# Turned q and k of the second half of the heads in two buffers, fetched two feature tiles ahead; apply of the first half three units behind the scores

## The chip, the core and the metric

The kernel runs on one core of one Trainium2 chip. The metric is the time of one execution on the device, in microseconds. The engines named below are TensorE (PE, matmuls), VectorE (DVE), ScalarE (ACT), GpSimd (POOL) and SyncE (SP); SP and POOL here mostly issue DMAs. Each engine takes its instructions in the order in which they stand in its own program, and waits at an instruction until the semaphores that it names have come.

## The reference

One layer of a hybrid encoder on 512 tokens of 1024 features, all in float32:

```python
x = x + 0.5 * swiglu(rmsnorm(x), w_ffn1)
h = rmsnorm(x)
xr, g, q, k, v, ga, gb = split(h @ w_in)        # 7 x 1024 columns
A = (rglru_forward(conv(xr)) + rglru_backward(conv(xr))) * gelu(g)
B = neighbourhood_attention(qk_norm(q), qk_norm(k), v, rpb)
x = x + (sigmoid(ga) * A + sigmoid(gb) * B) @ w_out
x = x + 0.5 * swiglu(rmsnorm(x), w_ffn2)
```

The attention has 16 heads of 64 features on a grid of 8 rows by 64 columns. A query sees all 8 rows and a window of 16 columns, with a learned bias `rpb`. The part that the change touches is this attention, and some buffers of the recurrent part (rglru).

## The kernel before

**Matmuls in three products.** Activations lie with features on partitions, 8 tiles of 128 features by 512 tokens. Each operand of a matmul is cut into a high and a low part (`split`, line 138 on), and a product is taken as high times high, low times high, high times low. A weight chunk is loaded by `load_w` (line 159): SP issues one DMA of 128x1024 floats into `wraw` (3 buffers, L163), ACT makes `wh` from it (L145) and DVE `wl` (L148, 4 buffers each), and PE then runs 24 matmuls of 512 columns on it (L172 to L174), 8 feature tiles by 3 products.

**Two kinds of work side by side.** The columns of the projection are computed chunk by chunk. Between the matmuls of a chunk generators ("lanes") are advanced at rates from the table `RATE`: `lru` for the recurrent part, `att` for the heads, `tail` for applies that are left over, `prep` for the norm of q and k, `v` for v. Within that a scheduler sets the final order on each engine by priority and by when a buffer is free. So a change of a buffer count moves instructions on every engine.

**The heads.** `heads(hf, ...)` handles half `hf` of the heads, 8 heads in 4 feature tiles `fi` of two heads each. For a tile, `start(fi)` makes `qh`, `ql`, `kh`, `kl` (ACT L960, DVE L962, ACT L963, DVE L965). `scores` runs the matmuls of q with k (PE L988), adds the bias and takes the maximum (DVE L1008), takes the exponential on ACT (L1015), the reciprocal of the sum (DVE L1017) and scales (ACT L1020). `ship` turns p on DVE (L1029, L1030) into `pt`, SP writes it to DRAM as `pd` (L1032), and POOL gathers it back, turned, into `PT` (L1036, four DMAs, 5 buffers). `apply` multiplies PT with v on PE (L1051) into a PSUM buffer, and ACT copies it out as `att` (L1061).

In half 0 a unit is half the columns of a tile (8 units), in half 1 a whole tile (4 units). `ATT_LAG` says how many units the apply of a tile stands behind its scores, 4 in half 0 and 2 in half 1; what is left at the end of a half goes to the lane `tail`.

**q and k of half 1** are normed in token layout, turned in blocks of 32 and written to DRAM as `qd` (L919). `fetch(qd, fi)` reads a tile back into `xqk` (four DMAs of SP, L932), which has one buffer: `fetch(0)` is called when `qd` is complete, and `start(fi)` calls `fetch(fi + 1)` behind the reads of tile fi. The buffers of the tags `xqk` and `PT` serve the recurrent part earlier in the program, for its cut inputs `ch` and `cl` (L728) and some of its `th` (L766); other `th` are in the common pool of large buffers.

**Around the change** PE runs the chunks of the columns for the gates (lines 1113 to 1124), which load from `wg`, and between them the scores and applies of both halves.

Of the kernel before, what the change touches and what calls it, by code (L numbers as in the profile page):

```python
# [9 lines left out]
F32 = mybir.dt.float32  # L10
F32R = mybir.dt.float32r
# [5 lines left out]
P = 128  # L17
T = 512
# [8 lines left out]
NCB, QC = 4, 16  # L27
# [33 lines left out]

GB_BATCH = (range(0, 4), range(4, 6), range(6, 7), range(7, 8))

ATT_LAG = 4, 2

LRU_PLAN = [
    ("root", range(4), range(39, 47)),
# [24 lines left out]
def block_kernel(ctx: ExitStack, tc, a, out):  # L92
# [4 lines left out]
    big = ctx.enter_context(tc.tile_pool(name="big", bufs=1))  # L97
# [10 lines left out]
    def nm(s):  # L108
        uid[0] += 1
        return f"{s}_{uid[0]}"  # L110
# [140 lines left out]
    def hold(i):  # L251

        after(i, mark["mm"])
        return i
# [454 lines left out]
    def lru():  # L709
        got, evicted, cuts, wts, fwd = {}, [], {}, {}, {}  # L710

        run = [None, None, None]

        def act(kind, i):
            hold(i)
            if kind == "tanh":
                kind = "exp" if run[0] == "sqrt" else run[0]
            if kind != run[0]:
                run[0], run[2] = kind, run[1]
            if run[2] is not None:  # L720
                after(i, run[2])
            run[1] = i

        def fetch(f):
            wts[f] = load_w(a["wgate"][f], 2 * P)

        def cut(f):
            cuts[f] = tuple(big.tile([P, T], F32R, tag="PT", bufs=5, name=nm(n)) for n in ("ch", "cl"))  # L728
            split(xc[f], *cuts[f])

        def gates(f):


            ps = [[aux_t() for _ in range(2)] for _ in range(2)]
            W, X = wts.pop(f), cuts.pop(f)
            mm = None
            for d in range(2):
                c = slice(d * P, (d + 1) * P)
                for w, x in ((0, 1), (1, 0), (0, 0)):
                    for b in range(2):  # L740
                        o = slice(b * HD, (b + 1) * HD)
                        prev, mm = mm, nc.tensor.matmul(  # L742
                            ps[d][b], W[w][o, c], X[x][o], start=x == 1, stop=w + x == 0)
                        if prev is not None:
                            after(mm, prev)
                        elif evicted:
                            after(mm, evicted[-1], True)
            for d in range(2):
                q = C_BG + f * 4 + d * 2
                both = pair_t()  # L750
                for b in range(2):
                    i = nc.scalar.activation(both[:, b], ps[d][b], AF.Sigmoid, bias=small[:, q + b : q + b + 1])
                    act("sigmoid", i)
                evicted.append(i)

                r, ix = (big_t(n="gate") for _ in range(2))
                for g, t in enumerate((r, ix)):
                    for b in range(2):
                        nc.gpsimd.dma_start(t[b * HD : (b + 1) * HD], both[g * HD : (g + 1) * HD, b])
                got[f, d] = r, ix  # L760

        def use(f, d):
            r, ix = got[f, d]
            hold(nc.vector.tensor_tensor(ix, ix, xc[f], ALU.mult))
            if d == 1 and f < 3:
                th = big.tile([P, T], F32, name=nm("th"), **(dict(tag="xqk", bufs=1) if f == 0 else dict(tag="PT", bufs=5)))  # L766
            else:
                th = big_t(n="th")
            act("tanh", nc.scalar.activation(th, r, AF.Tanh, scale=sp4[:, f * 2 + d : f * 2 + d + 1]))
            got[f, d] = r, ix, th  # L770


        def decay(f, d):
            r, ix, _ = got[f, d]
            act("exp", nc.scalar.activation(r, r, AF.Exp, scale=sn8[:, f * 2 + d : f * 2 + d + 1]))
            nc.vector.scalar_tensor_tensor(ix, r, 1.0, ix, ALU.add, ALU.mult)

        def root(f, d):
            _, ix, th = got[f, d]
            act("sqrt", nc.scalar.activation(th, th, AF.Sqrt))  # L780
            nc.vector.tensor_tensor(ix, ix, th, ALU.mult)

        def scan(f, d):
            av, ix, th = got.pop((f, d))
            if d == 0:
                fwd[f] = th
                i = hold(nc.vector.tensor_tensor_scan(th, av, ix, 0.0, ALU.mult, ALU.add))
            else:
                i = hold(nc.vector.tensor_tensor_scan(th[:, ::-1], av[:, ::-1], ix[:, ::-1], 0.0, ALU.mult, ALU.add))
            if "kl" in mark:  # L790
                after(i, mark["kl"])
            if d == 1:
                nc.vector.tensor_tensor(fwd[f], fwd[f], th, ALU.add)
                A[f] = fwd[f]

        plan = {}
        for fn, fs, steps in LRU_PLAN:
            units = list(fs) if fn in ("fetch", "cut", "gates") else [(f, d) for f in fs for d in range(2)]
            for u, step in zip(units, steps, strict=True):
                plan.setdefault(step, []).append((fn, u))  # L800
        do = dict(fetch=fetch, cut=cut, gates=gates, use=use, decay=decay, root=root, scan=scan)
        for step in range(max(plan) + 1):
            for fn, u in plan.get(step, []):
                do[fn](*(u if isinstance(u, tuple) else (u,)))
            yield
# [93 lines left out]
    def norm_qk(raws, st, qd):  # L899

        rq = tiny.tile([P, 2, NCB, 8], F32, tag="rq", name=nm("rq"))
        for w in range(2):
            for j in range(NCB):
                hold(nc.vector.tensor_scalar(rq[:, w, j, :], st[:, w, j, :], 1.0 / HD, epsv[:, j : j + 1],
                                             ALU.mult, ALU.add))
        hold(nc.scalar.activation(rq, rq, AF.Sqrt))
        nc.vector.reciprocal(rq, rq)
        yield
        for j in range(NCB):
            for w in range(2):  # L910
                t = raws[w][j].rearrange("p (h d) -> p h d", d=HD)
                hold(nc.vector.tensor_tensor(t, t, rq[:, w, j, :].unsqueeze(2).to_broadcast([P, 8, HD]), ALU.mult))
            if qd is not None:
                t2 = pair_t().rearrange("p a b -> p (a b)")
                for w in range(2):
                    nc.vector.transpose(
                        t2.rearrange("p (c f w i) -> p w f c i", c=NCB, f=4, w=2)[:, w],
                        raws[w][j].rearrange("p (f c i) -> p f c i", c=NCB, i=32))
                nc.sync.dma_start(qd[j], t2)  # L919
                yield  # L920
            elif j % 2 == 1:
                yield
        if qd is not None:
            yield
            fetch(qd, 0)

    xs = {}

    def fetch(qd, fi):
        t = xs[fi] = big.tile([P, NCB * NCB, 2, 32], F32, tag="xqk", bufs=1, name=nm("xqk"))  # L930
        for c in range(NCB):
            nc.sync.dma_start(  # L932
                t[c * 32 : (c + 1) * 32].rearrange("p g w i -> p g (w i)"),
                qd.rearrange("j (a i) c f x -> c f i (j a) x", a=NCB)[c, fi])

    def heads(hf, raws, qd):
# [6 lines left out]
        def start(fi):  # L943
# [19 lines left out]
            hold(nc.scalar.activation(k_of(kh), xk, AF.Copy))  # L963
            with tc.high_priority():
                mark["kl"] = nc.vector.tensor_tensor(k_of(kl), xk, k_of(kh.bitcast(F32)), ALU.subtract)  # L965
            if hf == 1 and fi < 3:
                fetch(qd, fi + 1)
            grid = lambda t: t.rearrange("p (r c) -> p r c", r=ROWS)
            qk[fi] = qh, ql, grid(kh), grid(kl)

# [52 lines left out]
        def ship(fi, n2):  # L1023

            outer, inner = soft.pop((fi, n2))
            t = big.tile([P, NCB, 7, 32], F32, tag="pt", bufs=2, name=nm("pt"))
            sub = lambda b, n: b[:, : n * P].rearrange("p (q c i) -> p q c i", q=n, i=32)
            to = t.rearrange("p c q i -> p q c i")
            nc.vector.transpose(to[:, 4:], sub(outer, 3))  # L1029
            nc.vector.transpose(to[:, :4], sub(inner, 4))  # L1030
            d = dram.tile([P, NCB, 7 * 32], F32, tag="pd", bufs=4, name=nm("pd"))
            nc.sync.dma_start(d, t.rearrange("p c q i -> p c (q i)"))  # L1032
            PT = big.tile([P, NCB, 7, 32], F32, tag="PT", bufs=5, name=nm("PT"))
            for c in range(4):
                q = slice(c * 32, (c + 1) * 32)
                nc.gpsimd.dma_start(PT[q].rearrange("p j q i -> p j (q i)"), d.rearrange("(j i) c x -> c i j x", j=4)[c])  # L1036
            PTs[fi, n2] = PT.rearrange("p a q i -> p q a i")

# [61 lines left out]
    for hf in range(2):  # L1100
        st = tiny.tile([P, 2, NCB, 8], F32, tag="st", name=nm("st"))
        raws = [qk_raw(0, hf, st), qk_raw(1, hf, st)]
        if hf == 1:
            qd = dram.tile([NCB, P, NCB, 4, 64], F32, name="qd")
# [152 lines left out]
```

## Time and profile before

| | us |
|---|---|
| median of 3 runs | 1110.05 |
| lowest and highest run | 1109.37, 1110.4 |
| the profiled execution | 1108.49 |
| its span, first to last instruction | 1106.7 |
| PE busy | 1093.7 |
| DVE, ACT, POOL busy | 796.1, 619.1, 140.1 |
| DMA, mean over the span | 163 GB/s |

A row of a timeline gives the start and the duration in us, the engine, the line, the operation, what it writes `<-` what it reads, and the count; in brackets at the end stands the idle time of the engine before it and what ended it. The page of waits sums those brackets by the waiting line and its releaser. The granted clock of PE is 1.000.

### The profile page before, as it was taken

The numbers are of one execution on the slowest core, as the hardware profiler recorded it, in microseconds if no ns is written. First come the engines' busy times: TensorE is split into PE (matmuls) and PEld (weight loads), VectorE is DVE, ScalarE is ACT, GpSimd is POOL, SyncE is SP. The second block draws the span as 40 slices with busy tenths as digits, with TensorE's granted clock in tenths as the row PEclk, the third lists the DMA queues.
The fourth block names the chain that finished last, engine by engine and source line by source line (L and its number), as shares of the span: only waits on it lengthen the run. The fifth ranks groups of instructions, "written<-read, shape, count | busy, mean of one in ns | idle before, by whom it ended". The sixth has DMA issues, their size and how long they took to land.

```text
span 1106.7 us, 17673 instructions
## 1 busy us (share of the span) xinstructions
PE 1093.7 (99%) x6779; PEld 969.0 (88%) x6779; DVE 796.1 (72%) x1228; ACT 619.1 (56%) x950; POOL 140.1 (13%) x243
## 2 busy tenths in 40 slices
PE   9999999999999999999999899999999999999998
PEld 7899999988888778787877778889999999998887
DVE  7877777795745786998886664659877777784642
ACT  8554544464443668777778673456655454464430
POOL 0000000000000342231325430001000000000000
PEclk9999999999999999999999999999999999999999
DMA  8576656643423576573799973477665666653421
GB/s 268 153 172 153 148 158 160 165 153 96 134 81 105 163 231 172 157 225 111 222 281 256 270 219 97 131 227 163 184 164 149 165 166 146 151 167 96 133 76 39
DMA packets 68452, 180.02 MB, mean 163 GB/s; under 512 B 17681, under 2 KB 21265, under 8 KB 68369
## 3 DMA queue, kind: packets, MB, share of 16 engines
q1 hardware_dynamic: 52160, 131.94, 36.8%
q0 software_dynamic: 15632, 46.70, 21.5%
q8 instruction: 53, 0.87, 0.3%
q10 hardware_dynamic: 576, 0.26, 0.1%
q14 instruction: 31, 0.25, 0.1%
HBM read 152.63 MB, written 17.83 MB: 154 GB/s over the span
## 4 chain that ended last, share of the span: by engine, by line
PE 95%; DMA 1%; DVE 1%; ACT 1%; issue 1%; SPq 0%; ACTq 0%; DVEq 0%
PE acc L312 31%; PE acc L172 11%; PE acc L173 10%; PE acc L174 10%; PE aux L312 5%; PE acc L834 4%; PE aux L172 4%; PE aux L174 4%; PE aux L173 4%; PE acc L835 4%; PE acc L836 4%; PE aux L1051 1%; PE aux L742 1%; PE aux L988 1%; DMA vd<-v 1%
## 5 line engine op out<-in xcount | busy, mean ns | idle before, releaser
L145 ACT ACTIVATE wh<-wraw 128x1024 fp32r<-128x1024 f32 (+3 forms) x236 | 233.4, 991 | 321.6 <-issue 90.5
L148 DVE TENSOR_TENSOR wl<-wraw,wh 128x1024 fp32r<-128x1024 f32 (+3 forms) x236 | 267.6, 1137 | 99.5 <-ACT wh L145 95.9
L312 PE MATMUL acc<-s,wh 128*128 128x256 f32 x1280 | 232.2, 283 | 0.0
L312 PEld LDWEIGHTS acc<-s,wh 128*128 128x128 f32 x1280 | 199.7, 192 | 0.0
L312 PE MATMUL acc<-s,wl 128*128 128x256 f32 x640 | 181.2, 283 | 0.0
L312 PEld LDWEIGHTS acc<-s,wl 128*128 128x128 f32 x640 | 122.9, 192 | 0.0
L172 PE MATMUL acc<-xh,wh 128*128 128x512 f32 x272 | 107.7, 396 | 0.0
L174 PE MATMUL acc<-xh,wl 128*128 128x512 f32 x272 | 106.3, 391 | 0.0
L173 PE MATMUL acc<-xl,wh 128*128 128x512 f32 x272 | 106.0, 390 | 0.0
L312 PE MATMUL acc<-xl,wh 128*128 128x256 f32 x320 | 90.6, 283 | 0.0
L312 PE MATMUL acc<-xh,wl 128*128 128x256 f32 x320 | 90.6, 283 | 0.0
L312 PE MATMUL acc<-xh,wh 128*128 128x256 f32 x320 | 90.6, 283 | 0.0
L834 PE MATMUL acc<-wh,xh 128*128 128x512 f32 x192 | 75.7, 394 | 1.0 <-ACT qk L846 1.0
L148 DVE TENSOR_TENSOR hl<-h,hh 128x512 fp32r<-128x512 f32 x88 | 57.3, 687 | 25.4 <-PE aux L173 24.2
L835 PE MATMUL acc<-wh,xl 128*128 128x512 f32 x192 | 74.8, 390 | 0.0
L836 PE MATMUL acc<-wl,xh 128*128 128x512 f32 x192 | 74.8, 389 | 0.0
L172 PE MATMUL aux<-hh,wh 128*128 128x512 f32 (+1 forms) x181 | 69.9, 386 | 0.0
L173 PE MATMUL aux<-hl,wh 128*128 128x512 f32 (+1 forms) x181 | 69.9, 386 | 0.0
L174 PE MATMUL aux<-hh,wl 128*128 128x512 f32 (+1 forms) x181 | 69.9, 386 | 0.0
L174 PE MATMUL acc<-hh,wl 128*128 128x512 f32 (+1 forms) x176 | 68.0, 386 | 0.0
L173 PE MATMUL acc<-hl,wh 128*128 128x512 f32 (+1 forms) x176 | 68.0, 386 | 0.0
L172 PE MATMUL acc<-hh,wh 128*128 128x512 f32 (+1 forms) x176 | 67.9, 386 | 0.0
(226 smaller groups left out, 2281.8 us busy)
## 6 DMA issues: line engine op xcount, KB each, us to landing
wraw<-wqkv SPq DMA_DIRECT2D x24, 512.0 KB
wraw<-wg SPq DMA_DIRECT2D x24, 512.0 KB
wraw<-w1d SPq DMA_DIRECT2D x22, 512.0 KB
wraw<-w2s SPq DMA_DIRECT2D x22, 512.0 KB
pair<-w2s SPq DMA_DIRECT2D x22, 512.0 KB
wraw<-w2d SPq DMA_DIRECT2D x22, 512.0 KB
wraw<-w1s SPq DMA_DIRECT2D x18, 512.0 KB
pair<-w1s SPq DMA_DIRECT2D x18, 512.0 KB
```

What stands on the lines that cost most here:

```text
L145: nc.scalar.activation(H, raw, AF.Copy)
L148: return nc.vector.tensor_tensor(L, raw, H.bitcast(F32), ALU.subtract)
L172: nc.tensor.matmul(ps, wh, xh, start=first, stop=False, skip_group_check=skip)
L173: nc.tensor.matmul(ps, wh, xl, start=False, stop=False, skip_group_check=skip)
L174: mark["mm"] = nc.tensor.matmul(ps, wl, xh, start=False, stop=last, skip_group_check=skip)
L312: mm = nc.tensor.matmul(o, w_[:, c], x_, start=first and m + k == 0 and w_ is H and x_ is xh_, stop=m + k == 4 and w_ is L, skip_group_che ...
L742: prev, mm = mm, nc.tensor.matmul(ps[d][b], W[w][o, c], X[x][o], start=x == 1, stop=w + x == 0)
L834: nc.tensor.matmul(pss[j], xh[kk][:, tj], H[:, s], start=kk == 0, stop=False)
L835: nc.tensor.matmul(pss[j], xl[kk][:, tj], H[:, s], start=False, stop=False)
L836: mark["mm"] = nc.tensor.matmul(pss[j], xh[kk][:, tj], L[:, s], start=False, stop=kk == KT - 1)
L988: mm = hold(nc.tensor.matmul(ps[hp][:, cs], q_[o, n * P : (n + 1) * P], keys(k_[o]), start=k_ is kl, stop=q_ is ql))
L1051: mm = nc.tensor.matmul(pv[h2 * HD : (h2 + 1) * HD, n * P : (n + 1) * P], vt[:, (fi * 2 + h2) * HD : (fi * 2 + h2 + 1) * HD], PT[:, q], st ...
```

## The change

The first half applies three units behind its scores in place of four. `xqk` gets a second buffer, and the buffers of `PT` go from five to four. `fetch` is called for tiles 0 and 1 when `qd` is complete, and in `start(fi)` for tile `fi + 2`. In the recurrent part `th` of the backward direction takes a buffer of `xqk` for f of 0 and 1 (before 0 alone) and of `PT` for 2 and 3 (before 1 and 2).

```diff
-ATT_LAG = 4, 2
+ATT_LAG = 3, 2
...
-            cuts[f] = tuple(big.tile([P, T], F32R, tag="PT", bufs=5, name=nm(n)) for n in ("ch", "cl"))
+            cuts[f] = tuple(big.tile([P, T], F32R, tag="PT", bufs=4, name=nm(n)) for n in ("ch", "cl"))
...
-            if d == 1 and f < 3:
-                th = big.tile([P, T], F32, name=nm("th"), **(dict(tag="xqk", bufs=1) if f == 0 else dict(tag="PT", bufs=5)))
+            if d == 1 and f < 4:
+                th = big.tile([P, T], F32, name=nm("th"), **(dict(tag="xqk", bufs=2) if f < 2 else dict(tag="PT", bufs=4)))
...
             fetch(qd, 0)
+            fetch(qd, 1)
...
-        t = xs[fi] = big.tile([P, NCB * NCB, 2, 32], F32, tag="xqk", bufs=1, name=nm("xqk"))
+        t = xs[fi] = big.tile([P, NCB * NCB, 2, 32], F32, tag="xqk", bufs=2, name=nm("xqk"))
...
-            if hf == 1 and fi < 3:
-                fetch(qd, fi + 1)
+            if hf == 1 and fi < 2:
+                fetch(qd, fi + 2)
...
-            PT = big.tile([P, NCB, 7, 32], F32, tag="PT", bufs=5, name=nm("PT"))
+            PT = big.tile([P, NCB, 7, 32], F32, tag="PT", bufs=4, name=nm("PT"))
```

From line 926 on, a line of the changed kernel is one higher than the same line before.

The change moves instructions at three places. The first is SP in the second half of the heads. In these rows `wraw` is the weight load of a chunk, `xqk` the fetch of q and k (5866 is tile 0; 6144 and 6149 are the ones that follow in their kernels), and `pd` the write of a transposed block of p. Before, from the load for the chunk behind the scores of tile 1 on:

```order
L163 DMA wraw_6479<-wg 128x1024
L932 DMA xqk_5866<-qd 32x16x64
L1032 DMA pd_5838<-pt_5835 128x896
L932 DMA xqk_5866<-qd 32x16x64 x3
L1032 DMA pd_5943<-pt_5940 128x896
L163 DMA wraw_6511<-wg 128x1024
L163 DMA wraw_6543<-wg 128x1024
L163 DMA wraw_6714<-wg 128x1024
L1032 DMA pd_6057<-pt_6054 128x896
```

After, the end of the same stretch (pd_6239 and pd_6249 are those of tile 0, pd_6437 and pd_6447 those of tile 1):

```order
L933 DMA xqk_5871<-qd 32x16x64 x4
L1033 DMA pd_5967<-pt_5964 128x896
L1033 DMA pd_6062<-pt_6059 128x896
L933 DMA xqk_6149<-qd 32x16x64 x4
L1033 DMA pd_6239<-pt_6236 128x896
L1033 DMA pd_6249<-pt_6246 128x896
L933 DMA xqk_6264<-qd 32x16x64 x4
L1033 DMA pd_6437<-pt_6434 128x896
L1033 DMA pd_6447<-pt_6444 128x896
L163 DMA wraw_6530<-wg 128x1024
L163 DMA wraw_6562<-wg 128x1024
L163 DMA wraw_6714<-wg 128x1024
```

The second load behind wraw_6479 (wraw_6511, now wraw_6530) has moved past the fetches of tiles 1 to 3 and six of the blocks of p; it stood ahead of the scores of tile 0 and stands behind both blocks of tile 1.

The second place is PE at the same point: what follows the scores of tile 1 (kl_6254 before, kl_6259 after). Before:

```order
L988 MATMUL acc_6363<-kh_6253,ql_6252 128x256
L172 MATMUL acc_6478<-xh_3088,wh_6480 128x512
...
L174 MATMUL acc_6478<-xh_3102,wl_6481 128x512
L172 MATMUL acc_6510<-xh_3088,wh_6512 128x512
L173 MATMUL acc_6510<-xl_3089,wh_6512 128x512
L174 MATMUL acc_6510<-xh_3088,wl_6513 128x512
```

After:

```order
L989 MATMUL acc_6368<-kh_6258,ql_6257 128x256
L172 MATMUL acc_6478<-xh_3088,wh_6480 128x512
...
L174 MATMUL acc_6478<-xh_3102,wl_6481 128x512
L1052 MATMUL aux_6510<-PT_5969,va_4899 64x128 x2
...
L1052 MATMUL aux_6510<-PT_6064,ve_4909 64x128 x2
L172 MATMUL acc_6529<-xh_3088,wh_6531 128x512
L173 MATMUL acc_6529<-xl_3089,wh_6531 128x512
L174 MATMUL acc_6529<-xh_3088,wl_6532 128x512
```

One chunk stands behind the scores in both; then an apply has come in ahead of the chunk whose weights are wraw_6530 (wraw_6511 before).

The third place is PE in the first half, around its first apply (PT_5277). In the rows L949 and L951 (one higher after) transpose the next q and k into `aux`, of which there are four PSUM buffers. Before, the apply stands behind the scores that follow those transposes:

```order
L949 MATMUL aux_5714<-ident,qk_4441 128x128
...
L951 MATMUL aux_5715<-ident,qk_4632 128x8x16
L172 MATMUL acc_5744<-xh_3088,wh_5746 128x512
...
L988 MATMUL aux_5782<-kh_5531,ql_5530 128x256
L1051 MATMUL aux_5816<-PT_5277,va_4899 64x128 x2
```

After:

```order
L989 MATMUL aux_5670<-kh_5531,ql_5530 128x256
L1052 MATMUL aux_5704<-PT_5277,va_4899 64x128 x2
...
L1052 MATMUL aux_5704<-PT_5393,ve_4909 64x128 x2
L950 MATMUL aux_5733<-ident,qk_4441 128x128
```

The first apply has moved ahead of the transposes, past one chunk and one block of scores. The second apply has moved in the same way, from behind the last scores of the first half to ahead of the chunk and a half before them.

## The prediction

> **What bounds the kernel now.** I read the page first, then the waits of TensorE (PE), then its timeline and that of SyncE (SP, which issues most DMAs) around the second half of the heads.
>
> ```profile
> PE 1093.7 (99%) x6779; PEld 969.0 (88%) x6779; DVE 796.1 (72%) x1228; ACT 619.1 (56%) x950; POOL 140.1 (13%) x243
> ...
> PEclk9999999999999999999999999999999999999999
> ...
> PE 95%; DMA 1%; DVE 1%; ACT 1%; issue 1%; SPq 0%; ACTq 0%; DVEq 0%
> ```
>
> PE is busy 99% of 1106.7 us and carries 95% of the chain that ended last. The change adds and removes no matmul. So its worth is the sum of the waits of PE that it takes away, less those that it makes. The page of waits names what there is to take:
>
> ```profile
> PE aux L988 <- DVE kl L965: 5.7, 3, 2.8
> PE aux L1051 <- DVE ql L962: 1.3, 1, 1.3
> ```
>
> The columns are the sum in us, how often, and the longest. In the timeline of PE a bracket at a row's end gives the idle time before it:
>
> ```profile
> 551.65 0.48 PE L172 MATMUL acc<-xh,wh 128*128 128x512 f32 x1
> 557.29 0.39 PE L988 MATMUL aux<-kl,qh 64*128 64x256 f32 x2
> 559.54 0.44 PE L1051 MATMUL aux<-PT,va 128*64 128x128 f32 x4 [1.26 <-DVE ql L962]
> 561.44 0.50 PE L172 MATMUL acc<-xh,wh 128*128 128x512 f32 x1
> 593.10 0.39 PE L988 MATMUL aux<-kl,qh 64*128 64x256 f32 x2
> 594.77 0.50 PE L172 MATMUL acc<-xh,wh 128*128 128x512 f32 x1
> 609.56 0.38 PE L988 MATMUL aux<-kl,qh 64*128 64x256 f32 x2 [1.48 <-DVE kl L965]
> 630.63 0.38 PE L988 MATMUL aux<-kl,qh 64*128 64x256 f32 x2 [2.78 <-DVE kl L965]
> 632.30 0.44 PE L1051 MATMUL aux<-PT,va 128*64 128x128 f32 x4
> 648.61 0.39 PE L988 MATMUL aux<-kl,qh 64*128 64x256 f32 x2 [1.47 <-DVE kl L965]
> ```
>
> The four rows of L988 at 593.10, 609.56, 630.63 and 648.61 are the scores of the feature tiles 0 to 3 of the second half; tiles 1, 2 and 3 wait for kl, 1.48 + 2.78 + 1.47 = 5.73 us. The row at 559.54 is the first apply, which waits 1.26. These rows also give PE's prices: a weight chunk of 24 matmuls takes 557.29 - 551.65 = 5.64, an apply 561.44 - 559.54 = 1.90, the scores of a tile of the second half 594.77 - 593.10 = 1.67.
>
> **What goes.** With two xqk buffers the q and k of a tile are in place one tile earlier, and the order of ScalarE (ACT) and VectorE (DVE) puts their qh, kh, ql and kl inside the softmax before. All three kl waits go: -5.73. The first apply now stands ahead of the transposes for the next q and k, so it no longer waits for a PSUM buffer that ql has to release: -1.26. Together **-6.99**. That is all that PE can gain here; the next waits in the list lie outside this stretch.
>
> **What comes: a weight load that stands behind the softmax.** The order of SP shows it. Before, the load of the chunk that follows (wraw_6511) goes out ahead of the transposed scores of tile 0; now its successor (wraw_6530) stands behind both transposed score blocks of tile 1 (pd_6437, pd_6447). SP takes its DMAs in order, and a pd waits until DVE has transposed p. The rows of SP before:
>
> ```profile
> 583.44 7.18 SPq L163 DMA_DIRECT2D wraw<-wg  x3
> 607.42 0.32 SPq L1032 DMA_DIRECT2D pd<-pt  x1
> 607.84 0.69 SPq L163 DMA_DIRECT2D wraw<-wg  x1
> 632.95 0.33 SPq L1032 DMA_DIRECT2D pd<-pt  x1
> 640.18 3.37 SPq L1032 DMA_DIRECT2D pd<-pt  x2
> 655.55 3.38 SPq L1032 DMA_DIRECT2D pd<-pt  x2
> ```
>
> The first row is wraw_6511 and the next two loads, issued at 583.44, some 26 us before the scores of tile 1. The others give the second pd of each tile; in a row x2 it starts about 0.33 before the row's end. After the start of its tile's scores it goes out 607.42 - 593.10 = 14.3 us (tile 0), 632.95 - 609.56 = 23.4 (tile 1), 643.2 - 630.63 = 12.6 (tile 2), 658.6 - 648.61 = 10.0 (tile 3). Of these 23.4 is no guide: there three weight loads stand on SP ahead of that tile's first pd, and the new order has none between these pd. Tile 2 is the nearest row, since the next q and k are made inside its softmax as they are now inside tile 1's: I take **12.6**, with 10.0 and 14.3 as ends.
>
> What follows on the load:
>
> ```profile
> 8.54 4.25 DMA wraw<-w1gu
> ...
> 418.76 0.33 SPq L163 DMA_DIRECT2D wraw<-wqkv  x1
> ...
> 424.22 1.06 ACT L145 ACTIVATE wh<-wraw 128x1024 fp32r<-128x1024 f32 x1 [0.19 <-DMA wraw<-wqkv]
> ...
> L145 ACT ACTIVATE wh<-wraw x20: 1045/1061/1063, 559.8 to 694.7; 128x1024 fp32r<-128x1024 f32 x20
> L148 DVE TENSOR_TENSOR wl<-wraw,wh x20: 1203/1225/1227, 561.3 to 695.8; 128x1024 fp32r<-128x1024 f32 x20
> ```
>
> From a pd to the next issue 607.84 - 607.42 = 0.42. A load that ACT waited for took 424.22 - 418.76 = 5.46 from issue to wh; the chain of waits shows another of 4.25. Then wh 1.06. A chunk's third matmul needs wl, 1.23 after wh, of which the first two matmuls cover two of 24 parts of 5.64, 0.47: 0.76 more. Ready after the scores' start: 12.6 + 0.42 + 5.46 + 1.06 + 0.76 = 20.3. PE has, between that start and this chunk, the scores (1.67), one chunk whose weights are there (5.64) and one apply (1.90): 9.2. **The wait is 20.3 - 9.2 = 11.1**; with 10.0 and 4.25 it is 7.3, with 14.3 it is 12.8. PE takes its matmuls in order, so nothing fills it: behind that chunk stand the next chunk and the scores of tile 2. The loads after it follow 0.42 apart, and each chunk gives 5.64 for a wh and a wl, so they are late only once.
>
> **What comes: less time ahead of tile 0.**
>
> ```profile
> 570.78 0.49 PE L172 MATMUL acc<-xh,wh 128*128 128x512 f32 x1
> 579.18 0.39 PE L988 MATMUL aux<-kl,qh 64*128 64x256 f32 x2
> 580.10 0.44 PE L1051 MATMUL aux<-PT,va 128*64 128x128 f32 x4
> 581.99 0.50 PE L172 MATMUL acc<-xh,wh 128*128 128x512 f32 x1
> ...
> 591.31 0.68 DVE L965 TENSOR_TENSOR kl<-xqk,kh 128x512 fp32r<-128x512 f32 x1
> ```
>
> The second apply (580.10, 1.89 long) stood between the last scores of the first half (579.18) and tile 0's (593.10); now it stands ahead of both, where the chunk at 570.78 resumed. From the last scores to kl, which DVE makes behind their softmax, 591.99 - 579.18 = 12.8 went by; PE now has 593.10 - 579.18 - 1.89 = 12.0. The same instructions stand in that stretch on ACT and DVE, so kl is late by **0.8** (ends 0 and 1.8; 1.11 was the cover).
>
> The second apply also comes 580.10 - 570.78 + 1.26 = 10.6 earlier and needs PT:
>
> ```profile
> 548.63 3.12 SPq L863 DMA_DIRECT2D vd<-v  x4
> ...
> 555.11 0.51 ACT L1015 ACTIVATE p<-so,nmx 128x256 f32<-128x256 f32 x1 [2.12 <-DMA vd<-v]
> ...
> 563.52 1.64 POOL L1036 DMA_DIRECT2D PT<-pd  x3 [0.16 <-issue]
> ...
> DMA to landing us min/median/max: 2.6/5.4/8.0
> ```
>
> The last of its gathers went out at about 564.6 and by the median 5.4 landed at 570.0, where PE now wants it at 569.5: 0.5 at the least. The new order puts att of the first apply on ACT ahead of the p of that unit, and att waits for the third of the four vd copies; the first ended ACT's wait at 555.11, and copies go out 3.12 / 4 = 0.8 apart, so some 1.6 + 0.6 for att, 2.2, would be added: 2.7 at the most. I take **1.5**.
>
> **What costs nothing.** Four buffers of PT instead of five put the last cut of the recurrent part just ahead of the last root on ACT:
>
> ```profile
> 455.86 0.61 ACT L780 ACTIVATE th<-th 128x512 f32<-128x512 f32 x1
> ...
> 457.29 0.68 DVE L148 TENSOR_TENSOR cl<-xc,ch 128x512 fp32r<-128x512 f32 x1
> ...
> 463.68 0.50 PE L742 MATMUL aux<-cl,wh 64*128 64x512 f32 x2
> ```
>
> Its cl ended at 457.97 already and is wanted at 463.68; 5.7 of cover for one ch. The four xqk DMAs more up front delay the next two pd on SP, whose applies stand over 20 us later. The fourth th in xqk or PT changes a place, not an operation: 0.
>
> **Sum.** -6.99 + 11.1 + 0.8 + 1.5 = **+6.4**. On the profiled execution, 1108.49 (1.79 outside the span), that is 1114.9; it stands 1.56 under the median of the runs, 1110.05, which gives **1116.5**. With the low ends (7.3, 0, 0.5) +0.8, 1110.9; with the high ends (12.8, 1.8, 2.7) +10.3, 1120.4.
>
> **Rivals.**
> *The change does what it says, and the weights are in time.* Then -6.99 + 0.8 + 1.5 = -4.7, **1105.4**. It decides at 9.2 - 0.42 - 5.46 - 1.06 - 0.76 = 1.5 us after tile 1's scores: were wraw_6530 issued by then, no wait would be left. For it speaks only that the buffer is free by then; against it the four rows of pd, none under 10.0. Chance 0.09.
> The Trainium skill, "DMA: Bandwidth & Descriptors", section "Issuing engines are not separate DMA queues", says that issuing from several engines "will only save the time on the sequencer it takes to initiate the DMA". By that a place behind two pd would cost their issue alone, and the time would be this rival's. SP's rows speak against it here: the second pd of a tile stands 10.0 us and more behind its scores because it waits, and a load behind it waits with it.
>
> *Gain and loss cancel.* Softmax of tile 1 runs as tile 3's did and the load as the fast one (7.3), and the applies wait for nothing: +0.3, **1110.4**. For it: ACT and DVE lose the wh and wl that stood in that softmax. Chance 0.09.
>
> *PE comes back at a slower pace after an idle stretch of 11 us.* The trace has none so long; after 1.48 to 2.78 of idle the scores still took 1.67 (632.30 - 630.63), as at 593.10 without a wait, and PEclk is 9 in every slice. If the first chunk after it took double, 5.64 more: **1122.1**; chance 0.12 for anything of that kind.
> The Trainium skill, "TensorE: Matmul & The Clock Gate", section "What's actually happening", has the clock halve after an idle window of about 3.4 us until as long a busy one has passed; by that figure it would be an estimated 1.7 us more.
>
> *The softmax of tile 1 is slower than any row taken,* as its 23.4 of before: 21.9 in place of 11.1, **1127.3**. Chance 0.05.
>
> **How the numbers follow.** My forecast, 1116.5 with 1110.9 to 1120.4 as its own ends, has the rest, 0.65. The range is **1110.5 to 1121.0**: below it lie the first rival and half of the second, above it the last and part of the third, about 2 in 10. Measurements of this kernel tell 0.2%, 2.2 us, from no change: faster is the first rival, 0.09; within it the second and the lowest end of the forecast, 0.10; slower the rest, 0.81.
>
> **What would show it.** In the profile of the changed kernel: no wait of L988 for kl at tiles 1 and 2, and none of the first apply for ql; one wait of 7 to 13 us of L172 for wh of L145 (or the DMA of wraw) between the scores of tiles 1 and 2, with wraw issued straight behind a pd; a wait under 2 of tile 0's scores for kl, and one of about 1.5 of the second apply for PT. If L172 waits less than 3 us there, the main step is wrong. If that wait is there and the chunk after it takes over 6, the third rival holds.

## The result, and the profile after

| | before | after |
|---|---|---|
| median (lowest to highest), us | 1110.22 (1109.37 to 1111.56) | 1117.57 (1117.43 to 1117.64) |
| ratio, 95% interval | | 1.0065 (1.0047 to 1.0082) |
| the profiled execution | 1108.49 | 1117.62 |
| its span | 1106.7 | 1115.8 |

The change makes the kernel slower by 7.35 us in the medians and by 9.1 between the two profiled executions. That these two differ is part of the explanation below. Three single executions among the runs below ran in a slow state (1347.03 us of before, 1805.53 of e5, 2798.11 of e8) and are left out of every median, range and count. The page after, with the busy times, the granted clock of PE in 40 slices and the chain that ended last:

```profile
PE 1096.9 (98%) x6779; PEld 971.5 (87%) x6779; DVE 796.1 (71%) x1228; ACT 619.1 (55%) x950; POOL 140.0 (13%) x243
...
PEclk9999999999999999999999799999999999999999
...
PE 93%; DVE 3%; ACT 2%; DMA 2%; issue 1%; SPq 0%; DVEq 0%; ACTq 0%
```

The same 6779 matmuls were busy 3.2 us longer, PE has 93% of the chain where it had 95%, and one slice of the clock has a 7 among the nines. PE's waits after (sum, times, longest):

```profile
PE acc L172 <- ACT wh L145: 10.8, 1, 10.8
PE aux L1052 <- issue: 1.9, 1, 1.9
PE aux L138 <- DVE pol L667: 1.1, 1, 1.1
PE acc L834 <- ACT qk L846: 1.0, 1, 1.0
PE aux L989 <- DVE kl L966: 0.3, 1, 0.3
```

Of the waits for kl and ql, 6.99 before, 0.3 is left. One wait of 10.8 for weights and one of 1.9 of the second apply have come; the page names no releaser for the second ("issue"), and the same wait is put down to PT in e1, e2 and e4. PE's timeline after, at the scores of the tiles 0, 1, 2 and 3 of the second half and at the chunk that waits:

```profile
594.47 0.40 PE L989 MATMUL aux<-kl,qh 64*128 64x256 f32 x2 [0.32 <-DVE kl L966]
...
609.14 0.39 PE L989 MATMUL aux<-kl,qh 64*128 64x256 f32 x2
...
629.25 0.80 PE L172 MATMUL acc<-xh,wh 128*128 128x512 f32 x1 [10.78 <-ACT wh L145]
...
640.42 0.39 PE L989 MATMUL aux<-kl,qh 64*128 64x256 f32 x2
...
655.09 0.39 PE L989 MATMUL aux<-kl,qh 64*128 64x256 f32 x2
```

What PE waited for at 629.25 is read on SP and ACT:

```profile
619.75 2.75 SPq L1033 DMA_DIRECT2D pd<-pt  x2
622.55 20.34 SPq L163 DMA_DIRECT2D wraw<-wg  x8
...
628.14 1.06 ACT L145 ACTIVATE wh<-wraw 128x1024 fp32r<-128x1024 f32 x1 [6.59 <-DMA wraw<-wg]
```

The second pd of tile 1 went out at 622.2, 13.0 after its scores; the load followed at 622.55, and wh began 5.59 after that. Then the first rows of the chunk, with the granted clock around them (columns: stretch, its length, PE, PEld, DVE, ACT, POOL busy with counts, clock, DMA share, GB/s):

```profile
629.25 0.80 PE L172 MATMUL acc<-xh,wh 128*128 128x512 f32 x1 [10.78 <-ACT wh L145]
...
632.39 0.63 PE L172 MATMUL acc<-xh,wh 128*128 128x512 f32 x1
...
634.88 0.39 PE L172 MATMUL acc<-xh,wh 128*128 128x512 f32 x1
...
637.61 0.39 PE L172 MATMUL acc<-xh,wh 128*128 128x512 f32 x1
```

```profile
620.00:621.00 1.00, 0.00 (x0) 0.00 (x0) 0.65 (x3) 1.00 (x4) 0.00 (x0) 1.00 1.01 322
621.00:622.00 1.00, 0.00 (x0) 0.00 (x0) 1.00 (x3) 0.56 (x2) 0.00 (x0) 0.57 1.06 277
622.00:629.00 7.00, 0.00 (x0) 0.00 (x0) 2.52 (x5) 0.86 (x1) 2.36 (x5) 0.50 0.98 352
...
632.00:634.00 2.00, 2.00 (x6) 1.61 (x5) 0.91 (x1) 1.04 (x1) 0.00 (x0) 0.50 1.02 231
634.00:635.00 1.00, 1.00 (x4) 0.77 (x3) 0.95 (x1) 0.02 (x1) 0.00 (x0) 0.60 1.03 224
635.00:636.00 1.00, 1.00 (x6) 0.82 (x5) 0.28 (x1) 0.00 (x0) 0.00 (x0) 1.00 1.04 230
```

PE stopped at 618.5. At about 621.1 its clock halved, and it stayed halved until about 634.8, 5.5 us after PE had resumed: matmuls of 0.39 took 0.63. The 24 matmuls of the first chunk took 637.61 - 629.25 = 8.36 in place of 5.64. From 629.25 to tile 2's scores at 640.42 the chunk and a half took 11.17, where the same number of matmuls took 569.84 - 561.44 = 8.40 before.

### The profile page after: what moved, and what is told of

The parts are those of the page before. It is cut to its first block, busy times and chain, and to the rows that moved or that the text cites. A ratio compares the mean times of both kernels' runs of the same rounds, so it can differ in the third digit from the quotient of the medians.

```text
span 1115.8 us, 17664 instructions
## 1 busy us (share of the span) xinstructions
PE 1096.9 (98%) x6779; PEld 971.5 (87%) x6779; DVE 796.1 (71%) x1228; ACT 619.1 (55%) x950; POOL 140.0 (13%) x243
## 4 chain that ended last, share of the span: by engine, by line
PE 93%; DVE 3%; ACT 2%; DMA 2%; issue 1%; SPq 0%; DVEq 0%; ACTq 0%
PE acc L312 31%; PE acc L172 10%; PE acc L174 9%; PE acc L173 9%; PE aux L312 5%; PE acc L834 4%; PE aux L173 4%; PE aux L172 4%; PE aux L174 4%; PE acc L835 4%; PE acc L836 4%; PE aux L742 1%; PE aux L1052 1%; DMA vd<-v 1%; ACT p L1021 1%
## 5 line engine op out<-in xcount | busy, mean ns | idle before, releaser
L172 PE MATMUL acc<-xh,wh 128*128 128x512 f32 x272 | 108.6, 399 | 10.8 <-ACT wh L145 10.8
L172 PEld LDWEIGHTS acc<-xh,wh 128*128 128x128 f32 x272 | 51.7, 190 | 23.7 <-ACT wh L145 11.0
```

Source lines behind the costliest of these rows:

```text
L172: nc.tensor.matmul(ps, wh, xh, start=first, stop=False, skip_group_check=skip)
```

## The experiments

All are compared with the kernel before, run beside them (medians 1109.2 to 1109.4). Beside the medians the mean granted clock of each execution matters, since it splits the executions of one kernel in groups. A code cut shows only the lines that matter; `after(a, b)` puts instruction a behind b.

**e1: the weights early again.** In the changed kernel three loads are tied to the place behind the fetch of tile 1 (the first line below stands in `fetch`):

```diff
+            mark["xqk", fi] = nc.sync.dma_start(
...
-        ld = nc.sync.dma_start(raw[:, s], src[:, s])
+        early = 73 <= nld[0] < 76
+        with tc.high_priority() if early else nullcontext():
+            ld = nc.sync.dma_start(raw[:, s], src[:, s])
+        if early:
+            after(ld, mark["xqk", 1])
```

> The changed kernel, with three weight loads (wraw_6530 and the two behind it) put on SP straight behind the fetch of tile 1, ahead of the pd of the second half; nothing else is edited. Theory (the loss is the load that stands behind the softmax, and the slow pace of PE behind that wait): the wait of L172 for wh, 10.8, is gone, the chunk and a half behind it take 8.4 in place of 11.2, granted clock 1.00 throughout: 1117.6 - 10.8 - 2.8 = 1104.0, up to 1105.6 if tile 3's kl is then late. Rival (the second buffer or the later fetches cost by themselves, and the load is only where the wait shows): another wait of similar size takes its place, 1112 to 1118.

Measured: 1106.05 (1105.33 to 1107.68, 8 executions), ratio 0.9974 (0.9965 to 0.9984). The three loads now go out at 587.33, the wait for wh is gone, and the loss with it. What is left of PE's new waits:

```profile
PE aux L1056 <- DMA PT<-pd: 2.4, 1, 2.4
...
PE acc L178 <- DVE wl L148: 0.5, 1, 0.5
PE acc L468 <- DVE wh L453: 0.5, 1, 0.5
PE aux L993 <- DVE kl L970: 0.3, 1, 0.3
```

So the load was the main cause. The median missed the 1104.0 by 2 and lies 0.45 above the upper end of 1105.6: the second apply waits 0.5 longer than in the changed kernel, and the two waits of 0.5 are new. Four executions at a clock of 1.000 took 1105.33 to 1106.37 (a fifth, at 0.999, 1105.43), three at 0.998 took 1107.21 to 1107.68. The profiled one is among these three, and in it the clock halves behind the wait of the second apply:

```profile
572.77 0.66 PE L1056 MATMUL aux<-PT,vs 128*64 128x128 f32 x8 [2.40 <-DMA PT<-pd]
```

```profile
573.00:578.00 5.00, 5.00 (x27) 3.96 (x24) 2.39 (x10) 4.33 (x10) 1.24 (x3) 0.66 1.05 316
```

**e2: the lag alone.** Before, with one number changed:

```diff
-ATT_LAG = 4, 2
+ATT_LAG = 3, 2
```

> Before, with ATT_LAG 3 for the first half and nothing else (one xqk buffer, five PT). Theory (the second buffer moved the load, not the lag): the load keeps its early place on SP; the 1.3 of the first apply goes, the second apply waits about 1.9 for PT as in the changed kernel, the three kl waits of 5.7 stay: 1110.2 - 1.3 + 1.9 = 1110.8, between 1109 and 1112.5. Rival (the earlier applies moved the load): the wait for wh shows up here, 1119 to 1122.

Measured: 1117.18 (1115.43 to 1118.44), ratio 1.0076 (1.0063 to 1.0089). Neither theory had this, and the median lies above the range that was given: the load kept its early place and no wait for wh appeared, and yet the time is that of the whole change. Its waits, then the clock behind the second apply and behind one of the waits for kl:

```profile
PE aux L988 <- DVE kl L965: 6.9, 3, 3.4
PE aux L1051 <- DMA PT<-pd: 2.6, 1, 2.6
...
PE aux L988 <- ACT att L1061: 0.7, 1, 0.7
```

```profile
571.00:580.00 9.00, 6.41 (x51) 5.22 (x48) 6.78 (x19) 8.16 (x15) 4.38 (x8) 1.00 1.00 330
...
614.00:618.00 4.00, 3.94 (x28) 3.53 (x29) 0.01 (x1) 1.12 (x2) 0.00 (x0) 0.57 1.03 313
```

Against before, the waits for kl are 1.2 longer, the second apply waits 2.6 and att 0.7 more, and the 1.3 of the first apply is gone, in sum 3.2. The span grew by 7.0. Two waits for kl are now over 3 us (3.18 and 3.44), and behind each the clock is halved for about 3.4 us of work, 1.7 lost twice. That gives 6.6 of the 7.0. I had counted waits alone. This is the profiled execution, the shortest of the five; the others, at 0.992 to 0.995, were not traced, and why the waits for kl grew was not followed.

**e3: the buffers alone.** The change without its first line (`ATT_LAG = 4, 2` stays).

> Before, with the second xqk buffer, the fetch two tiles ahead, four PT and the places of th, but ATT_LAG 4 as before. Theory (the second buffer moves the load): the three kl waits go, -5.7; the load stands behind both pd of tile 1, and since no apply stands between tile 1's scores and the chunk here, the wait is 20.1 - 7.3 = 12.8, and PE is slow for some 2.8 behind it: 1110.2 - 5.7 + 12.8 + 2.8 = 1120.1, between 1118 and 1122. Rival (the lag moved it): 1104 to 1106.

Measured: 1116.75 (1116.63 to 1118.47), ratio 1.0073 (1.0061 to 1.0085). So it is the buffers and not the lag that move the load, as the order of SP shows and as this wait confirms:

```profile
626.86 0.80 PE L172 MATMUL acc<-xh,wh 128*128 128x512 f32 x1 [11.70 <-ACT wh L145]
```

The median lies 1.3 below the low end that I gave. The wait is 1.1 shorter than expected, and the first apply waits 0.6 in place of 1.3; that makes 1.8 of the 3.4 by which the 1120.1 is missed. The other 1.6 is the size of the offset between the profiled execution of before and its median, which my sum, started from the median, carried over (see the last step below). Of the four parts of this edit (the second `xqk` buffer, the earlier fetches, the buffers of `PT`, the places of `th`) none was run alone; that it is the second `xqk` buffer with its earlier fetches is read from the order of SP, not shown by a run. Each half of the change alone costs about 7, and both together cost no more: with the second buffer the kl waits that the lag lengthens are not there.

**e4: something to do in the wait.** The changed kernel with 42 matmuls on constants between the apply, whose last matmul is `mark["pv"]`, and the chunk that waits:

```diff
+        if nld[0] == 73 + 1:
+            ps0 = aux_t()
+            for i in range(42):
+                f0 = nc.tensor.matmul(ps0[:, :P], ones, ones, start=True, stop=True)
+                after(f0, mark["fill" if i else "pv"])
+                mark["fill"] = f0
...
+            mark["pv"] = mm
```

> The changed kernel, with 42 matmuls of 128x128 on constants (not used) put on PE between the apply and the chunk that waits for its weights; at 0.227 each (16 of them took 3.63 at the start of the span of before) they fill 9.5 of the 10.8 of idle time. Theory (PE ran at half its clock in the wait and for 5 us behind it): the clock stays at 1.00, the chunk and a half behind the wait takes about 9.2 (8.4 and 0.8 for wl) in place of 11.2, the wait itself is the same: 1117.6 - 2.0 = 1115.6. Rival (the slow rows behind the wait are wl and the other late weights): no gain, 1117.6, or slower by what the fillers overshoot.

Measured: 1115.96 (1114.17 to 1119.08, 6 executions); the median falls between two groups of three. In the profiled one, of the lower group (1114.17 to 1114.43), the clock is 1.00 throughout:

```profile
628.02 0.50 PE L172 MATMUL acc<-xh,wh 128*128 128x512 f32 x1 [0.48 <-ACT wh L145]
629.28 0.50 PE L176 MATMUL acc<-xh,wl 128*128 128x512 f32 x1 [0.53 <-DVE wl L148]
...
637.22 0.39 PE L997 MATMUL aux<-kl,qh 64*128 64x256 f32 x2
```

The weights are still late (the chunk starts 19.4 after tile 1's scores, 20.1 in the changed kernel), and the chunk and a half took 9.20, as worked out, in place of 11.17: 2.0 of the loss was the clock. The other three, at 0.997 to 0.998, took 1117.5 to 1119.1 and were not traced; why they lie more than one half-clock stretch above the lower group stays open.

**e5: the buffers of the change, lag 4, and the weights early.** e3 with the edit of e1.

> The buffers of the change with ATT_LAG 4 as before (e3), and the three weight loads straight behind the fetch of tile 1 (as in e1). Theory (the gain of the second buffer is real, and what costs is the load behind the softmax and the second apply that comes too early for its PT): no wait for wh, no wait of an apply for PT, no kl wait over 0.5, clock 1.00 in every execution: e3's 1116.75 - 11.7 - 2.8 = 1102.3, between 1101 and 1104, faster than before and than every run so far. Rival (the waits that go come back elsewhere): 1105 or more.

Measured: median 1103.60 (1103.36 to 1105.37, 4 executions), ratio 0.9950 (0.9936 to 0.9963): faster than both kernels, by 5.7 against before, and by more against the change. The waits of its profile:

```profile
PE aux L138 <- DVE pol L671: 1.1, 1, 1.1
PE acc L838 <- ACT qk L850: 1.0, 1, 1.0
PE aux L1056 <- DVE ql L967: 0.8, 1, 0.8
PE acc L178 <- DVE wl L148: 0.6, 1, 0.6
```

None is over 1.1, and the clock is 1.000 in each of the four executions. The median stands 1.3 above the estimate, of which the two last rows are 0.8, measured against what e3 had.

**e6 to e10: how long PE may stand idle.** A stop of chosen length in e5, ahead of the fourth chunk of the output projection, where nothing else waits (n memsets: 3, 5, 9, 0, 1):

```diff
+            f0 = nc.tensor.matmul(g0[:, :P], ones, ones, start=True, stop=True)
+            after(f0, mark["mm"])
+            with tc.high_priority():
+                nc.vector.tensor_copy(g1[:, :P], g0[:, :P])
+                for _ in range(n):
+                    nc.gpsimd.memset(g1, 1.0)
...
+            f1 = nc.tensor.matmul(g2[:, :P], g1[:, :P], g1[:, :P], start=True, stop=True)
+            mark["fill"] = f1
```

The next chunk stands behind `f1`.

> The kernel of e5 with a stop of PE put ahead of the fourth chunk of the output projection: a small matmul, a copy by DVE, three memsets of 0.55 by POOL, and a small matmul that reads them; an idle stretch of about 2.4 where nothing else waits. Theory (the clock halves after an idle stretch somewhere between 2.4 and 3.2, and stays so for about 3.4 of work, 1.7 lost): in some executions the clock stays at 1.00 and the time is e5 + 2.9, in others 1.7 more. Rival (the drop comes from what the chip does in the heads, not from idle time): e5 + 2.9 in all.

> As e6 with five memsets, an idle stretch of about 3.5. Theory: the clock halves behind it in all or nearly all executions: e5 + 4.0 + 1.7 = e5 + 5.7. Rival: e5 + 4.0.

> As e6 with nine memsets, an idle stretch of about 5.7. Theory: as e7, and the loss does not grow with the stretch: e5 + 6.2 + 1.7 = e5 + 7.9 in all executions. Rival: e5 + 6.2.

> As e6 without a memset: PE waits for the copy by DVE alone, which by e6's trace ended 2.8 after PE's last matmul, so an idle stretch of about 2.8. If the clock halves at a fixed length between 2.6 and 3.2 of idle time, all executions read alike, e5 + 3.3 (1106.9) without a drop or e5 + 4.7 with one. If it depends on where the stretch falls in a running window, both kinds come among the executions, some 1.4 apart.

> As e6 with one memset, an idle stretch of about 3.7. With a drop in every execution: e5 + 3.7 + 0.6 + 1.3 = e5 + 5.6 = 1109.2. If the drop needs over 4 of idle time: 1107.9.

The stops came out longer than meant in e6 to e8, since the copy stood behind other work of DVE. The rows of the matmul that reads the copy or memset, in e9 and e10:

```profile
731.60 0.49 PE L1173 MATMUL aux<-gap 128*128 128x128 f32 x2 [2.82 <-DVE gap L1169]
```

```profile
731.76 0.79 PE L1173 MATMUL aux<-gap 128*128 128x128 f32 x2 [3.48 <-POOL gap L1171]
```

| | idle in the profiled execution, us | median, us | span of the profiled execution less that of e5 (1102.0) | clock of the executions |
|---|---|---|---|---|
| e9 | 2.82 | 1108.72 | 3.6 | 5 of 12 at 1.000, 7 at 0.997 or 0.998 |
| e10 | 3.48 | 1109.76 | 5.2 | all of 11 at 0.997 or 0.998 |
| e6 | 5.04 | 1112.08 | 8.5 | all of 9 at 0.997 or 0.998 |
| e7 | 6.53 | 1112.93 | 8.4 | all of 7 at 0.997 or 0.998 |
| e8 | 8.16 | 1115.72 | 10.0 | all of 4 at 0.995 to 0.997 |

The two added matmuls cost about 0.7. In e9's profiled execution, clock 1.000, 2.82 and 0.7 make the 3.6. Those of e10, e7 and e8 have 1.0 to 1.2 more, e6 2.8 (1.2 of it a wait for ql that is longer there): the drop costs 1 to 1.6 and does not grow with the stop. The clock shows how long it lasts, here in e10 and in e7:

```profile
730.00:736.00 6.00, 4.24 (x13) 3.52 (x14) 1.65 (x4) 0.68 (x2) 1.46 (x2) 0.72 0.76 192
```

```profile
730.00:740.00 10.00, 4.95 (x17) 4.12 (x18) 1.88 (x4) 0.91 (x2) 3.55 (x6) 0.66 0.54 129
```

A mean of 0.72 over 6 us is 6 x 0.28 / 0.5 = 3.4 us at half the clock, and 0.66 over 10 us is 6.8. The traces have halved stretches of 3.4 us (e1, both of e2, e10), of 6.8 (e6, e7, e8) and of 13.7 (the changed kernel, e3), and no other lengths.

In e9 both kinds come among the executions: 1106.31 to 1107.74 at a clock of 1.000, and 1108.69 to 1111.52 below it. Only one of the first kind was traced; that the stop halves the clock in the others follows from e5, which lacks the stop and has all four at 1.000. The single-length reading falls, and the traces show it by themselves: the clock halves behind 2.40 in e1 and stays at 1.00 behind 2.59 in e2, 2.78 in before and 2.82 in e9. The larger medians of e6 and e8 were not followed further.

## Why the prediction was right, and where it was not

Time, range and direction held (1117.57 against 1116.5). By its own steps:

- **The waits that go, 6.99.** This is shown: no wait of tiles 1 to 3 for kl is left and none of the first apply for ql.
- **The weight load behind the softmax, 11.1 with its wl.** This is shown in place, cause and size: pd went out 13.0 after the scores (12.6 taken), load to wh took 5.59 (5.46), and the wait is 10.78 where 10.3 and 0.8 for wl were worked out. e1 removes it by an edit of the loads alone (behind tile 2 two later applies also came out in two parts); e3 shows that the buffers of the change moved the loads, and not the lag.
- **Tile 0's kl, 0.8.** It measured 0.32: the term was too large, within its ends.
- **The second apply's PT, 1.5.** It measured 1.94, by the way that was given. ACT's rows after show the p of the second apply's unit behind an att that waited 2.63 for a vd copy:

```profile
558.68 0.60 ACT L1062 ACTIVATE att<-aux 128x512 f32<-128x512 f32 x1 [2.63 <-DMA vd<-v]
559.17 1.19 ACT L1021 ACTIVATE p<-p,rs 128x192 f32<-128x192 f32 x3
```

- **The pace of PE behind the wait, taken as nothing.** This is the step that failed. The third rival, given 0.12 and up to 5.64, did occur, by its own sign (the chunk took 8.36, over 6), and beside the forecast, not in its place. The chunk and a half took 11.17 in place of 8.40, of which e4 shows 2.0 to be the clock, and the 0.8 for wl was foreseen.
- **One offset between profile and median, 1.56.** I carried it over as if it were the same for both kernels. By all signs it is the clock again. Of 22 executions of before beside e9 and e10, six at 1.000 took 1107.50 to 1108.32 and sixteen at 0.998 or 0.996 took 1108.72 to 1111.27. The profiled execution of before was one without a drop; its median lies, by its time, in the group with one. The wait of 2.78 for kl is the one of the length at which e9 shows both kinds; that it is this wait which halves the clock was not traced, since the traced execution is one without.

The sum of the profiled spans then closes: -6.99 + 10.78 + 1.94 + 0.32 + 2.77 (the chunk and a half) + 0.07 (PE runs that much later by the scores at 549.87, now 549.94) = 8.89 of 9.1. In the medians the change also takes away before's own drop, some 1.6, which leaves about 7.3. So that the median came as close to 1116.5 as it did is luck: two omissions, 2.0 against the kernel and 1.6 for it, nearly cancelled. The size on the profiled executions, 6.4 against 9.1, was short by the clock above all.

The Trainium skill, "TensorE: Matmul & The Clock Gate", section "What's actually happening", has the clock halve after an idle window of about 3.4 us that runs free of the program. The traces agree in kind, by the 0.50 rows and by halved stretches of 3.4, 6.8 and 13.7 us, about one, two and four times 3.4. In the idle time that is enough they differ: 2.40 us in e1 and 3.18 in e2, both under 3.4.

## What to carry to other kernels

Before a buffer is added, read in the new order of the issuing queue what the extra transfers and their waits push back: a weight load behind one DMA that waits for a softmax is as late as that softmax, however free its own buffer is. A faster supply that shifts two orders at once is worth taking apart: here the buffers gain 5.7 once the loads are held in place, and the shorter lag only cost. Count a wait of the matrix engine of some 2.4 us or more with a slow stretch that may come behind it, and compare medians only after looking at the clock of each execution.

## What the runs showed of the hardware

The profiled executions show the granted clock halved behind idle stretches of PE of 2.40 us (e1), 3.18 and 3.44 (e2), 3.48 and more (e10, e6, e7, e8, the changed kernel, e3), and at 1.00 behind 1.94 (the changed kernel), 2.59 (e2), 2.78 (before) and 2.82 (e9). So between 2.40 and 2.82 the length alone does not decide. A halved stretch lasted 3.4, 6.8 or 13.7 us. In the changed kernel it began 2.6 us after PE stopped, lasted until 5.5 us after PE had resumed, and cost 2.0; behind the stops of e10, e7 and e8 it cost 1.0 to 1.2, whatever their length. Forty-two matmuls whose result nobody reads kept the clock at 1.00 through a wait of ten microseconds in the traced execution; three of the six executions with them were at 0.997 to 0.998.
